# A hybrid attention and expert layer on one core: the rope tables move behind the first latents, and the first projection's weights are split ahead of tiles 2 and 3

## Chip, cores and metric

The kernel runs on one core of one Trainium2 chip. The metric is the device time of one execution in microseconds, the median of several runs.

## What is computed

One decoder layer for 512 tokens of width 1024, in fp32. This is the reference, cut to what matters here:

```python
mod = silu(c) @ w_ada + b_ada                      # 6 x 1024: shift1, scale1, gate1, shift2, scale2, gate2
h = rms_norm(x, norm1_g) * (1 + scale1) + shift1
proj = h @ w_in                                    # columns: cq 384, ckv 256, kpe 32, fq, fk, fv 512 each, fl 8
q_a = rms_norm(cq, mla_qa_g) @ w_uq                # 8 heads of 64 + 32
k_nope, v_a = rms_norm(ckv, mla_kva_g) @ w_ukv
q_a, k_a = rms_norm(q_a), rms_norm(concat(k_nope, kpe))
q_a[..., 64:], k_a[..., 64:] = rope(...)           # angles = positions * inv_freq, cos and sin
o_a = causal attention(q_a, k_a, v_a)
o_b = causal attention(fq, fk, fv) with a forget-gate bias, cumsum(log_sigmoid(fl + b_f))
x = x + gate1 * (concat(o_a, o_b) @ w_o)
h2 = rms_norm(x, norm2_g) * (1 + scale2) + shift2
x = x + gate2 * peer(h2)                           # product keys 128 x 128, 16 experts for each of 8 heads
```

## The kernel before

The 512 tokens are four tiles of 128 rows (`T[0]` to `T[3]`). The kernel is written as generators, whose order of writing is the priority of their instructions; a scheduler then gives each engine a fixed order, in which every engine works strictly. Tiles of on-chip memory come from pools with a fixed number of buffers: `k4` 28 (rows, weights), `k3` 6 (`cl`, `lT`, `macc`, `rg`, `ropework` and others), `ld` 4, `g8` 2.

Start. `setup` makes constants. `mod_cols` makes the shift `b1` and the scale `a1` of the first norm, in halves of 512 columns: eight matmuls of `w_ada` (line 303), a copy to `macc` on ScalarE (line 304), eight small matmuls that turn the row into columns (line 318), and one or two additions on VectorE (lines 319, 321). `hidden(i)` loads 128 rows of `x`, squares and sums them on ScalarE (line 345), takes the reciprocal root on GpSimd (lines 127, 128), scales on VectorE (line 347), and after a pause transposes them on the tensor engine (line 136) and applies `a1` and `b1` to each 128x128 block, even blocks on ScalarE (line 167), odd ones on VectorE (line 165). `part` then splits the result into a high part `hTh`, a cast to a reduced fp32 format on ScalarE (line 397), and a low part `hTl`, the rest (line 398: the first half on VectorE, the second on GpSimd). Before the task list starts, `hidden(0)` and `hidden(1)` and the four halves of modulation are woven by hand.

`tables` makes small constants, loads gains, and at its end calls `rope_tables`: three transfers on ScalarE's queue (`pos`, `frq`, `rg`), VectorE work on a `k3` tile `ropework` (lines 245 to 264), two sines on ScalarE (line 265), and eight products with the gains `rg` into the table `rope` (lines 274 to 277). The tables are read by GpSimd in `mla_tile` (lines 503 to 514).

Projections. `w_in(name)` loads a weight in parts of two blocks of k on SP's queue (line 371) and splits each into `whi` (ScalarE, line 373) and `wlo` (VectorE, line 374); it does so once, at its first call, and later calls find the result. `times_h` multiplies in three passes for each of 8 blocks of k: high by high, high by low, low by high (lines 385 to 387). `latent_q` uses `w_c0` (384 columns) and makes `cl`; `latent_k` uses `w_c1` (296 columns), `fox_v`, and `fox_qk` twice, use 512 columns each; `mla_tile` follows.

Order. `pipe(tasks, 3)` starts one task a step and continues each live task every third step, the newest first. The list is `hidden(2)`, `hidden(3)`, then `base`, then the heads. From step 10 on, `mods` adds the other four modulation vectors between the steps; their `w_ada` loads of 1 MB use the two `g8` buffers and are issued behind the last weight load written before them.

After the projections come attention, output projection, second norm, the product-key search, and from about 480 us on two long loops over 128 blocks of experts (`dense_u`, `v_mm`), which take most of the time.

Of the kernel before, what the change touches and what calls it, by code (L numbers as in the profile page):

```python
# [78 lines left out]
class Layer:  # L79
# [126 lines left out]
    def tables(self):  # L206
        nc, cp, I = self.nc, self.cp, self.I
        v = nc.vector
        self.io = cp.tile([P, P], F32, name="io")
        nc.gpsimd.iota(self.io, pattern=[[1, P]], base=0, channel_multiplier=0, allow_small_or_imprecise_dtypes=True)  # L210
        self.io2 = cp.tile([P, NK, 2], F16, name="io2")
        v.tensor_copy(self.io2, self.io[:, :, None].to_broadcast([P, NK, 2]))


        self.qcol_a = cp.tile([QK, 1], F32, name="qcol_a")
        self.qcol_b = cp.tile([FD + 2, 1], F32, name="qcol_b")
        g = cp.tile([ND, 4], F32, name="gcols")
        nc.scalar.dma_start(g, I["gcols"])
        v.memset(self.qcol_a, -QK ** -0.5)
        v.memset(self.qcol_b, 1.0)  # L220
        v.memset(self.qcol_b[FD:FD + 1], -1.0)
        v.scalar_tensor_tensor(out=self.qcol_a[:ND], in0=g[:, 0:1], scalar=-QK ** -0.5, in1=g[:, 1:2],
                               op0=OP.mult, op1=OP.mult)
        v.scalar_tensor_tensor(out=self.qcol_b[:FD], in0=g[:, 2:3], scalar=-FD ** -0.5, in1=g[:, 3:4],
                               op0=OP.mult, op1=OP.mult)
        self.latg = cp.tile([P, 5], F32, name="latg")
        nc.scalar.dma_start(self.latg, I["lat_g"])
        self.bf = cp.tile([P, H], F32, name="bf")
        nc.scalar.dma_start(self.bf, I["b_f"].to_broadcast([P, H]))
        self.logf = [cp.tile([P, H], F32, name=f"logf{i}") for i in range(NT)]  # L230
        self.rope_tables()

    def rope_tables(self):
        nc, cp, I = self.nc, self.cp, self.I
# [765 lines left out]
    def build(self):  # L1000
# [17 lines left out]
        def seq(*gs):  # L1018
            for g in gs:
                yield from g  # L1020
# [9 lines left out]
        def spread(g, n):  # L1030
            for _ in g:
                for _ in range(n):
                    yield
# [5 lines left out]
        def prep(f, *a):  # L1039
            f(*a)  # L1040
            yield
# [9 lines left out]
        def gates(i):  # L1051
# [1 line left out]

        every = list(range(NT))
        each = lambda f, *a: [f(i, T[i], *a) for i in every]
        base = (each(self.latent_q) + each(self.latent_k) + each(self.fox_v) + each(self.fox_qk, 0)
                + each(self.fox_qk, 1) + each(self.mla_tile))
        hs = [self.hidden(i, T[i]) for i in every]
        for x in ("a1", "b1", "a2", "b2"):
# [3 lines left out]
        h0, h1 = hs[:2]  # L1063
        for g in (m[0], h0, h1, m[1], m[0], m[2], m[1], m[3], m[2], m[3], h0, h1):
            next(g, None)
        self.tables()
        mods = spread(seq(self.mod_row(2, 0, self.g1d), self.mod_cols(3, "b2", 2), self.mod_cols(4, "a2", 3, 5),
                          self.mod_row(5, 1, self.g2d)), 2)
# [87 lines left out]
```

## Time and profile before

| | before |
|---|---|
| median of 3 runs | 1693.03 us (1692.58 to 1693.55) |
| profiled execution, its own time | 1691.5 us |
| profiled execution, its span from first to last instruction | 1689.1 us |
| mean granted tensor clock | 0.979 |
| tensor engine busy | 1586.1 us, 94% of the span |
| VectorE busy | 1263.2 us, 75% |
| ScalarE busy | 678.6 us, 40% |
| GpSimd busy | 478.6 us, 28% |

The profile shows one execution. Times in it are microseconds from the span's start. PE is the tensor engine's matmuls and PEld its weight loads, DVE is VectorE, ACT ScalarE, POOL GpSimd, SP the queue that issues most loads. A timeline row gives the start, the time it lasts, the engine and line of code, the operation, what it writes and reads, and how many instructions were merged; in brackets, how long the engine had been idle and what ended that. A granted clock of 1.00 is 2.4 GHz, 0.50 is 1.2 GHz.

### The profile page before, as it was taken

Reading aid. Unit: us, or ns where it says so; the run is one execution under the profiler, and the core shown is the slowest. Engines: PE = TensorE matmul, PEld = TensorE weight load, DVE = VectorE, ACT = ScalarE, POOL = GpSimd, SP = SyncE. Lnnn points to the kernel's source line nnn. Section 1 sums busy time; section 2 is a strip of 40 time slices with the busy share of each in tenths; the row PEclk is TensorE's granted clock in tenths of the full one; section 3 lists DMA queues with packets and bytes.
Section 4 is the critical chain, followed back from the end, with each engine's and each line's share of the span. In section 5 each row is a group of like instructions: output and inputs, shape, how many; then the busy total and the mean of one; then the engine's idle time right before and its main releaser. Section 6 shows DMA issues by size and latency. Waiting matters only on the chain.

```text
span 1689.1 us, 25030 instructions
## 1 busy us (share of the span) xinstructions
PE 1586.1 (94%) x8993; PEld 1390.9 (82%) x8993; DVE 1263.2 (75%) x2626; ACT 678.6 (40%) x1072; POOL 478.6 (28%) x514
## 2 busy tenths in 40 slices
PE   5999999998978999999999999799999999999996
PEld 2976498987977999999999999787777777877885
DVE  2624364585899679899989899488888888887863
ACT  3522364354224434334656656333333333333331
POOL 1303510001013355564213232123333333233311
PEclk8999999999989999999999999999999999999998
DMA  7354513368154688888999999999999999999852
GB/s 295 122 212 159 194 39 132 121 215 272 36 188 139 229 287 264 262 281 270 346 335 337 328 325 349 387 354 368 353 370 357 366 365 358 366 375 364 289 180 100
DMA packets 189391, 451.34 MB, mean 267 GB/s; under 512 B 16594, under 2 KB 102610, under 8 KB 185172
## 3 DMA queue, kind: packets, MB, share of 16 engines
q1 hardware_dynamic: 91732, 277.17, 46.1%
q0 software_dynamic: 38656, 139.48, 23.5%
q10 hardware_dynamic: 58880, 33.11, 6.5%
q8 instruction: 70, 1.15, 0.3%
q14 instruction: 53, 0.43, 0.1%
HBM read 393.07 MB, written 56.63 MB: 266 GB/s over the span
## 4 chain that ended last, share of the span: by engine, by line
PE 75%; DVE 11%; DMA 7%; ACT 2%; issue 2%; POOL 0%; POOLq 0%; SPq 0%; DVEq 0%; ACTq 0%
PE acc L981 27%; PE bank L937 8%; PE bank L936 8%; PE bank L935 8%; PE bank L386 4%; PE bank L173 4%; PE bank L387 4%; PE bank L385 4%; DVE ulo L872 3%; PE bank L820 3%; DMA vt<-in_peer_v 2%; PE bank L136 2%; PE bank L564 2%; PE bank L579 2%; DMA ge<-ged 1%
## 5 line engine op out<-in xcount | busy, mean ns | idle before, releaser
L981 PE MATMUL acc<-vhi,whl 128*128 128x512 f32 x1536 | 422.6, 395 | 25.7 <-ACT vhi L871 17.0
L981 PEld LDWEIGHTS acc<-vhi,whl 128*128 128x128 f32 x1536 | 289.0, 189 | 94.1 <-ACT vhi L871 21.7
L937 PE MATMUL bank<-hhi,ulo 128*128 128x384 f32 x1024 | 348.0, 340 | 17.2 <-DVE ulo L872 17.2
L935 PE MATMUL bank<-hhi,uhi 128*128 128x384 f32 x1024 | 346.3, 339 | 12.3 <-ACT uhi L871 12.2
L936 PE MATMUL bank<-hlo,uhi 128*128 128x384 f32 x1024 | 348.3, 340 | 0.0
L831 POOL DMA_INDIRECT gat<-in_peer_v,ids x128 | 158.4, 1238 | 348.2 <-DVE y L859 324.2
L871 ACT CAST uhi<-ut 128x1024 fp32r<-128x1024 f32 x128 | 134.5, 1051 | 304.5 <-PE bank L936 262.4
L981 PE MATMUL acc<-vlo,whl 128*128 128x512 f32 x768 | 241.0, 395 | 0.1
L831 POOL DMA_INDIRECT gat<-in_peer_u,ids x128 | 142.6, 1114 | 336.0 <-DVE sact L849 305.1
L872 DVE TENSOR_TENSOR ulo<-ut,uhi 128x1024 fp32r<-128x1024 f32 x128 | 178.5, 1395 | 63.6 <-ACT uhi L871 62.8
L937 PEld LDWEIGHTS bank<-hhi,ulo 128*128 128x128 f32 x1024 | 194.3, 190 | 23.0 <-DVE ulo L872 22.6
L935 PEld LDWEIGHTS bank<-hhi,uhi 128*128 128x128 f32 x1024 | 194.3, 190 | 14.2 <-ACT uhi L871 13.8
L936 PEld LDWEIGHTS bank<-hlo,uhi 128*128 128x128 f32 x1024 | 194.5, 190 | 0.5
L872 DVE TENSOR_TENSOR vlo<-vt,vhi 128x1024 fp32r<-128x1024 f32 x128 | 156.4, 1222 | 43.6 <-ACT vhi L871 42.7
L871 ACT CAST vhi<-vt 128x1024 fp32r<-128x1024 f32 x128 | 133.7, 1049 | 110.6 <-PE acc L981 85.4
L981 PEld LDWEIGHTS acc<-vlo,whl 128*128 128x128 f32 x768 | 145.1, 189 | 33.1 <-DVE vlo L872 1.2
L859 DVE SCALAR_TENSOR_TENSOR y<-gat,swgt,y 128x1024 f32<-128x1024 f32 x127 | 167.8, 1322 | 1.8 <-DMA gat<-in_peer_v,ids 1.7
L971 ACT CAST whl<-ge 128x384 fp32r<-128x384 f32 x128 | 65.4, 512 | 257.4 <-PE acc L981 240.1
L849 DVE CUSTOM_DVE_ANT_0 scr<-gat,h2r 128x1024 bf16<-128x1024 f32 x128 | 166.2, 1298 | 0.1
L972 DVE TENSOR_TENSOR whl<-ge,whl 128x384 fp32r<-128x384 f32 x128 | 70.8, 555 | 55.6 <-ACT whl L971 52.4
L822 ACT ACTIVATE gst<-bank 128x512 f32<-128x512 f32 x96 | 96.8, 1117 | 9.3 <-PE bank L820 4.7
L968 DVE TENSOR_TENSOR ge<-ge,gt 128x384 f32<-128x384 f32 x128 | 69.8, 552 | 17.7 <-DMA ge<-ged 15.6
(252 smaller groups left out, 2217.2 us busy)
## 6 DMA issues: line engine op xcount, KB each, us to landing
ut<-in_peer_uT SPq DMA_DIRECT2D x128, 512.0 KB
vt<-in_peer_v SPq DMA_DIRECT2D x128, 512.0 KB
G<-gst ACTq DMA_DIRECT2D x24, 1024.0 KB
gt<-G SPq DMA_DIRECT2D x16, 1536.0 KB
ged<-ge SPq DMA_DIRECT2D x120, 192.0 KB
ge<-ged SPq DMA_DIRECT2D x120, 192.0 KB
w<-in_w_ada SPq DMA_DIRECT2D x16, 1024.0 KB
w<-in_w_pq SPq DMA_DIRECT2D x32, 512.0 KB
```

Of the source, the lines that this page charges most:

```text
L822: nc.scalar.activation(st[:, :, q + t4:q + t4 + 4].rearrange("p i t -> p t i"), pb.rearrange("p (t i) -> p t i", t=4), AF.Copy, scale=1.0 ...
L831: self.nc.gpsimd.indirect_dma_start(out=t, out_offset=None, in_=self.I[table], in_offset=bass.IndirectOffsetOnAxis(ap=ids[:, k:k + 1], axi ...
L849: v.tensor_tensor_reduce(out=scr, in0=u, in1=self.rows, op0=OP.mult, op1=OP.add, scale=1.0, scalar=0.0, accum_out=a[:, k:k + 1])
L859: v.scalar_tensor_tensor(out=self.y, in0=t, scalar=w[:, k:k + 1], in1=self.y, op0=OP.mult, op1=OP.add)
L871: nc.scalar.copy(hi, src)
L872: self.last_split = eng.tensor_tensor(out=lo, in0=src, in1=hi, op=OP.subtract)
L935: pe.matmul(A, uh[:, k, :], hh, start=(k == 0), stop=False)
L936: pe.matmul(A, uh[:, k, :], hl, start=False, stop=False)
L937: pe.matmul(A, ul[:, k, :], hh, start=False, stop=(k == KD - 1))
L968: nc.vector.tensor_tensor(out=wg, in0=wg, in1=self.gt[:, :, b % GI, :], op=OP.mult)
L972: nc.vector.tensor_tensor(out=wl, in0=w, in1=wh, op=OP.subtract)
L981: self.nc.tensor.matmul(self.acc[t][half], w[:, ts], v[:, half * 512:(half + 1) * 512], start=(b == n == 0), stop=(b == NK - 1 and n == 2))
```

## The change

Two moves, and no instruction is added or taken away. `tables` no longer calls `rope_tables`; instead it is one more task in the list, behind the four `latent_q` and before the four `latent_k` (`prep` makes a task of one step of a plain function). And `w_in("w_c0")`, the load and split of the first projection's weight, which the first `latent_q` did at its first call, is called before `tables` and so before the tasks of `hidden(2)` and `hidden(3)`. As the list has one task more, every later task starts one step later, while `mods` still begins at step 10.

```diff
@@ tables
         self.logf = [cp.tile([P, H], F32, name=f"logf{i}") for i in range(NT)]
-        self.rope_tables()
 
@@ build
         each = lambda f, *a: [f(i, T[i], *a) for i in every]
-        base = (each(self.latent_q) + each(self.latent_k) + each(self.fox_v) + each(self.fox_qk, 0)
+        base = (each(self.latent_q) + [prep(self.rope_tables)] + each(self.latent_k) + each(self.fox_v) + each(self.fox_qk, 0)
                 + each(self.fox_qk, 1) + each(self.mla_tile))
@@ build
             next(g, None)
+        self.w_in("w_c0")
         self.tables()
```

## Rows read from the trace of the kernel before

**Rows 1.** Page, busy time: us, share of the span, instructions.
```profile
PE 1586.1 (94%) x8993; PEld 1390.9 (82%) x8993; DVE 1263.2 (75%) x2626; ACT 678.6 (40%) x1072; POOL 478.6 (28%) x514
```

**Rows 2.** Stretches from 30 to 130 us: busy per engine, clock, DMA.
```profile
30.00:32.00 2.00, 1.32 (x10) 0.97 (x8) 1.83 (x10) 0.58 (x1) 0.00 (x0) 1.00 1.03 401
32.00:42.00 10.00, 0.15 (x2) 0.10 (x1) 3.58 (x20) 5.74 (x13) 3.23 (x4) 0.54 0.32 109
42.00:46.00 4.00, 3.63 (x13) 2.80 (x14) 3.25 (x5) 1.95 (x4) 1.30 (x2) 0.50 0.03 13
46.00:63.20 17.20, 17.20 (x103) 17.17 (x102) 9.80 (x17) 8.41 (x19) 5.57 (x8) 0.99 0.41 120
63.20:72.00 8.80, 8.80 (x66) 8.80 (x66) 3.18 (x5) 2.69 (x5) 0.74 (x2) 1.00 0.93 337
72.00:130.00 58.00, 57.03 (x296) 43.43 (x298) 22.91 (x99) 19.97 (x48) 9.33 (x26) 1.00 0.42 156
```

**Rows 3.** Waits of the tensor engine, 0 to 130 us: total, times, longest.
```profile
PE bank L385 <- ACT whi L373: 10.6, 2, 9.9
```

**Rows 4.** Timeline of the tensor engine: start, duration, line, idle before.
```profile
31.00 1.05 PE L318 MATMUL bank<-o,macc 128*128 128x1 f32 x8 [0.68 <-ACT macc L304]
41.90 1.01 PE L385 MATMUL bank<-whi,hTh 128*128 128x384 f32 x2 [9.85 <-ACT whi L373]
```

**Rows 5.** Timeline of ScalarE and its queue, 30 to 76 us.
```profile
30.37 0.33 ACTq L243 DMA_DIRECT2D rg<-in_rope_g  x1
...
33.57 0.40 ACT L265 ACTIVATE ropework<-ropework 128x64 f32<-128x64 f32 x2
33.86 0.80 ACT L167 ACTIVATE x<-bank,b,a 128x128 f32<-128x128 f32 x2
37.90 1.14 ACT L397 CAST hTh<-x 128x512 fp32r<-128x512 f32 x2 [3.24 <-DVE x L165]
38.94 1.05 ACT L345 ACTIVATE xn<-x 128x1024 f32<-128x1024 f32 x1
...
41.04 0.81 ACT L373 CAST whi<-w 128x768 fp32r<-128x768 f32 x1
...
63.23 0.49 ACT L419 ACTIVATE cl<-bank 128x384 f32<-128x384 f32 x1 [3.00 <-PE bank L387]
...
74.02 1.28 ACT L450 ACT_TABLE_LOAD   x1
```

**Rows 6.** Timeline of VectorE, 30 to 68 us.
```profile
30.14 0.64 DVE L249 TENSOR_SCALAR ropework<-frq,posf 128x16 f32<-128x16 f32 x4
...
32.79 0.29 DVE L264 TENSOR_SCALAR ropework<-ropework 128x64 f32<-128x64 f32 x2
...
36.38 0.22 DVE L276 SCALAR_TENSOR_TENSOR rope<-ropework,rg 128x64 f32<-128x64 f32 x1 [2.26 <-DMA rg<-in_rope_g]
...
37.47 0.72 DVE L165 TENSOR_SCALAR x<-bank,a,b 128x128 f32<-128x128 f32 x2
42.02 0.75 DVE L347 TENSOR_SCALAR xn<-x,nrs 128x1024 f32<-128x1024 f32 x1 [3.84 <-POOL nrs L128]
...
44.17 0.95 DVE L374 TENSOR_TENSOR wlo<-w,whi 128x768 fp32r<-128x768 f32 x1
...
65.30 2.59 DVE L374 TENSOR_TENSOR wlo<-w,whi 128x592 fp32r<-128x592 f32 x3
```

**Rows 7.** Timeline of SP's queue, loads issued.
```profile
20.80 1.67 SPq L281 DMA_DIRECT2D x<-in_x  x2
...
51.49 10.76 SPq L371 DMA_DIRECT2D w<-in_w_fv  x4
62.30 32.81 SPq L291 DMA_DIRECT2D w<-in_w_ada  x4
```

**Rows 8.** Timeline of GpSimd, the low halves of `hT`.
```profile
38.59 2.49 POOL L398 TENSOR_TENSOR hTl<-x,hTh 128x512 fp32r<-128x512 f32 x2 [23.24 <-ACT hTh L397]
...
49.70 1.77 POOL L398 TENSOR_TENSOR hTl<-x,hTh 128x512 fp32r<-128x512 f32 x1 [6.24 <-ACT hTh L397]
```

## Prediction

> **What bounds the kernel now.** I began with the page's busy times: the tensor engine is busy for 94% of the span [rows 1], so time can only be won where it stands still or runs at a low clock. The stretches by window then show where that is near the change. From 30 to 32 us it is at its full clock; from 32 to 42 us it works for 0.15 us in ten, with a granted clock of 0.54; from 42 to 46 it is busy again, but at 0.50, the 1.2 GHz level; from 46 us on it is full, at 0.99 to 1.00, up to 130 us and past it [rows 2]. So there is one hole of ten microseconds ahead of the first projection, and behind it a stream that has no room. The waits of the tensor engine up to 130 us say the same: the longest ends with the first high half of `w_c0`, 9.9 us [rows 3].
>
> I then read each engine through that hole, to see which one is late. The last modulation column is made by matmuls that end at 32.05 [rows 4]. ScalarE scales its half of the first two tiles' rows at 33.86 to 34.66 and then stands idle for 3.24 us until VectorE has scaled the other half [rows 5]. VectorE is late because rope work stands in front: it waits 2.26 us for the gains `rg`, does eight table products (36.38 to 37.47) and only then scales the two rows [rows 6]. The gains were asked for at 30.37 and used 6.0 us later [rows 5, 6]. After the casts of `hTh` (37.90 to 39.04) ScalarE takes the squares of tiles 2 and 3 from 38.94, and the first high half of `w_c0` only at 41.04 [rows 5]. VectorE makes the first low half at 44.17, behind the rows of tiles 2 and 3, which begin at 42.02 [rows 6]. Rope first and later tiles second: both stand on the path that sets the hole.
>
> **The rope tables move.** Leaving the old place are fourteen VectorE instructions between 30.14 and 33.08, eight from 36.38 to 37.47, two sines in 0.40 us on ScalarE [rows 5] and three small transfers on ScalarE's queue, `pos`, `frq` and `rg`. Both engines scale blocks of the same transposed rows, so VectorE's pair could start with ScalarE's at 33.86; I allow it half a microsecond for what else stands in its order, 34.35, where the trace has 37.47 [rows 5, 6]: 3.1 us earlier (3.6 at most). The casts of `hTh` follow at 34.8 in place of 37.90.
>
> At the new place, behind the fourth `latent_q`, the same work returns: 2.9 + 1.1 = 4.0 us at most on VectorE. It is busy for 3.18 of the 8.80 us from 63.2 to 72 and 9.80 of the 17.2 before [rows 2], so the cover is 5.6 or 7.4 us. The products queue in front of whatever VectorE has next, the low halves of `w_c1` from 65.30 [rows 6], and those feed the tensor engine. In addition `rg` and `ropework` share six buffers with four `cl` tiles, so I expect them to be asked for only after the fourth `cl` is begun, at 63.23 in the old time [rows 5]; a transfer like the old one then needs 6.0 us, as its new neighbours keep the DMA engines busy at 0.93 [rows 2]. The cost is nothing if the products stand behind the low halves, and up to 6.0 us if they stand in front and the tensor engine runs dry. I take nothing for the sum, because the empty VectorE time is larger than the work, and keep 6.0 for the range.
>
> **The split of `w_c0` moves.** Four loads of 0.39 MB, four casts of 0.81 us on ScalarE and four subtractions of 0.95 us on VectorE [rows 5, 6] now stand in front of tiles 2 and 3. On SP's queue the loads pass the two rows of 0.52 MB that are issued at 20.80 [rows 7]. At 401 GB/s [rows 2] that is 2.6 us: the DMA engines fall idle at about 34.7 (109 GB/s over the ten microseconds from 32 are 2.7 us at 401), so `w_c0` is complete at about 32.1 in place of 34.7, its first two parts by 30.1, and the rows of tiles 2 and 3 come by 34.7 in place of 30.8. They are read at 38.94 [rows 5], so that is hidden; without that cover it would be 3.9 us for those two tiles alone.
>
> What is won: the two squares no longer stand before the first cast, 41.04 - 38.94 = 2.1 us. The stretch from 42 to 46 holds 13 tensor instructions; at the pace of the next stretch (103 in 17.2 us, 0.167 each) they need 2.2 us, so 1.8 of its 4 us are the low clock and the wait for the first low half. These I count as won, since ScalarE and VectorE can make both before the tensor engine comes. Third, the first four k blocks of tiles 0 and 1 are ready at 30 us, 24 matmuls of 0.167 = 4.0 us that can run while the second half is scaled. How many do depends on whether ScalarE takes the casts while it waits for the last column or behind `hTh`: between nothing and 4.0 us, and I take half, 2.0.
>
> What it costs: tile 0 and 1's last low halves, two instructions of GpSimd in 2.49 us, took 1.77 us for one when VectorE subtracted at the same time [rows 8]. With `w_c0`'s subtractions beside them I take 3.5 in place of 2.5, a loss of 1.0 us. The Trainium skill (GPSIMD Engine Reference, Specifications) says that GpSimd shares its SBUF interfaces with VectorE and contends with instructions of two SBUF inputs, which `w_c0`'s subtractions are; by that the 1.0 us is to be expected, and the 1.77 us row agrees, whereas the 2.49 us row alone would give nothing.
>
> **The queue behind.** One task more in the list puts the gate row's first two `w_ada` loads of 1 MB in front of `w_fv`'s: 5.2 us at 401 GB/s. `w_fv` is issued from 51.49 to 62.25 and `w_ada` directly behind, at 62.30 [rows 7]. The DMA engines are busy for 0.41 of the stretch from 46 to 63.2 [rows 2], so ten microseconds are free: I cost it at nothing; without that cover 5.2 us.
>
> The sum is 3.1 + 2.1 + 1.8 + 2.0 - 1.0 = 8.0 us. Everything behind hangs on the tensor engine's stream [rows 2], so it passes to the end. The profiled execution took 1691.5 us for a span of 1689.1; less 8.0 that is 1683.5. It lies 1.5 us below the median of 1693.03, so I forecast 1685.0.
>
> Bounds: the first latent matmul can't start before 32.05, against 41.90 [rows 4], 9.85 us, and with the 1.8 us that is 11.7; some room for a different order later gives 13, or 1680. The least that stands alone is the rope's 3.1 us.
>
> **The rivals.**
>
> - *Tiles 2 and 3 are late.* Their squares now follow four casts and their rows four subtractions, 3.2 and 3.8 us. If the tensor engine is through with tiles 0 and 1 before they are ready, half of the gain goes: 4 us are left, 1689. For it: VectorE waits 3.84 us for the root that GpSimd makes for tile 2, at 42.02 [rows 6], and GpSimd's last low halves of tiles 0 and 1 stand before that root. Against: all of this chain starts earlier by the rope's 3.1 us too.
> - *Rope's wait only moves.* The gains come 6.0 us after the request, VectorE holds `w_c1`'s low halves behind the products, and the tensor engine waits: 8.0 - 6.0 = 2.0 us are left, 1691, no change that can be told.
> - *The same wait drags more with it: slower.* If 6.0 us of waiting, 4.0 of work and a restart at the low clock (1.8) fall on the path in full, 11.8 us are lost against 8.0 won: 1697. It decides from 8.0 us on. It needs the low halves of `w_c1` all behind the products; against it, the row at 65.30 holds three subtractions, so at least one of the four was made before the fourth `cl` in the old order [rows 6].
> - *The sines fall behind the first exponential.* The trace has them with no table load between the last modulation columns and themselves at 33.57, and the load for the exponential at 74.02, 1.28 us [rows 5]. Behind it they would take two more loads: 2.6 us, 5.4 left, 1687.6. Their place, ten microseconds ahead of it, speaks against. The Trainium skill (ScalarE: Activation LUTs, Table sets: the hidden batching unit) asks that functions of one table set be batched, and this change moves the sines away from theirs, so by its rule the risk is real; it puts a switch at about 2.66 us, which would make 5.3 for two.
>
> **How the numbers follow.** Forecast (6 to 12 us won) 0.58; tiles 2 and 3 late 0.13; rope's wait moves 0.14; slower 0.09; sines 0.06. A measurement of this kernel tells 0.2%, 3.4 us, from no change. Faster is the first, second and last, 0.77, with 0.01 more from the rope case: 0.78; same 0.13; slower 0.09. The range runs from 1680 to 1693, which leaves out the slower case and a little below.
>
> **What would show it.** The wait before the first `w_c0` matmul falls from 9.9 us to under 3; the clock in 32 to 46 us stays near 1; VectorE's scaling stands directly behind ScalarE's; the last `latent_q` square comes at about 55 in place of 63.23; the sines show no load of their own. The prediction is wrong if VectorE waits for `rg` in front of `w_c1`, if the tensor engine has a new hole before tile 2, or if the gain at 63 us is gone at 400.

## The result, and the profile after

The median after is 1704.68 us (1703.06 to 1706.11, four runs) against 1693.29 (1692.58 to 1693.71, four runs): a ratio of 1.0068 [1.0052, 1.0084], 11.4 us slower. The forecast was 1685.0 with a range of 1680 to 1693. The profiled execution took 1705.09 us for a span of 1703.0. All times below are from its trace or from the trace of the kernel that is named; behind `tables` a line number is one lower than before.

The page's span and its busy times, which answer to [rows 1]:

```profile
span 1703.0 us, 25028 instructions
...
PE 1598.0 (94%) x8993; PEld 1398.5 (82%) x8993; DVE 1261.7 (74%) x2626; ACT 679.5 (40%) x1072; POOL 480.8 (28%) x514
```

The counts are the same, and the tensor engine is busy 11.9 us longer: 2.7 of them at the weight `w_c1`, where its clock was lower (shown below), the others spread over the span. The stretches by window, in the columns of [rows 2] (busy time of PE, PEld, DVE, ACT, POOL, then granted clock, DMA share and GB/s), show where it stands still:

```profile
20.00:32.00 12.00, 12.00 (x70) 5.75 (x71) 2.63 (x9) 3.71 (x8) 0.00 (x0) 0.73 1.03 407
32.00:42.00 10.00, 8.12 (x42) 5.88 (x39) 6.01 (x13) 6.16 (x11) 2.94 (x2) 1.00 0.39 130
42.00:52.00 10.00, 4.60 (x28) 3.89 (x26) 4.72 (x9) 5.43 (x13) 3.70 (x9) 0.91 0.35 106
52.00:62.00 10.00, 9.83 (x46) 9.73 (x47) 3.82 (x9) 4.13 (x10) 3.30 (x4) 0.74 0.58 238
62.00:72.00 10.00, 5.12 (x25) 4.78 (x24) 6.96 (x27) 3.32 (x8) 0.74 (x2) 0.77 0.34 108
72.00:82.00 10.00, 10.00 (x68) 10.00 (x67) 0.02 (x1) 0.00 (x0) 0.00 (x0) 0.89 0.00 0
```

The one hole of 32 to 42 us is closed: 8.12 us busy in ten, at 1.00, where [rows 2] has 0.15 at 0.54. In its place stand two: 4.60 busy in ten from 42 us and 5.12 from 62 us, each with a clock of 0.74 to 0.77 where work begins again. In [rows 2] the stream was full from 46 us on. The waits of the tensor engine from 30 to 130 us (total, times, longest) name the two, as [rows 3] named the one:

```profile
PE bank L384 <- ACT whi L372: 5.9, 3, 4.9
PE bank L384 <- ACT hTh L396: 3.0, 1, 3.0
PE bank L136 <- DVE xn L346: 2.5, 1, 2.5
```

The 9.9 us wait for a `whi` is gone. New are the waits for the transposes' rows `xn` (2.5 us) and for `hTh` (3.0), which are tile 2's, and a 4.9 us wait for another `whi`, that of `w_c1`. The tensor engine's timeline, as in [rows 4]:

```profile
33.52 1.05 PE L317 MATMUL bank<-o,macc 128*128 128x1 f32 x8 [0.69 <-ACT macc L303]
34.43 0.60 PE L384 MATMUL bank<-whi,hTh 128*128 128x384 f32 x2
```

The first latent matmul follows the last modulation matmuls without a wait. The modulation itself was 2.5 us later in this execution (31.00 there, 33.52 here). I put that down to the clock of the first 32 us, which differs between traces even where the work up to there is the same (last section), so I measure from the last copy of a modulation row, `macc`: 30.36 before, 32.88 after. ScalarE and its queue, as in [rows 5]:

```profile
38.37 1.14 ACT L396 CAST hTh<-x 128x512 fp32r<-128x512 f32 x2 [0.64 <-DVE x L165]
39.41 1.56 ACT L372 CAST whi<-w 128x768 fp32r<-128x768 f32 x2
44.67 0.49 ACT L418 ACTIVATE cl<-bank 128x384 f32<-128x384 f32 x1 [3.69 <-PE bank L386]
...
45.15 1.05 ACT L344 ACTIVATE xn<-x 128x1024 f32<-128x1024 f32 x1
...
46.65 1.05 ACT L344 ACTIVATE xn<-x 128x1024 f32<-128x1024 f32 x1
...
64.00 0.49 ACT L418 ACTIVATE cl<-bank 128x384 f32<-128x384 f32 x1 [3.58 <-PE bank L386]
64.01 0.33 ACTq L242 DMA_DIRECT2D rg<-in_rope_g  x1
...
67.81 0.40 ACT L264 ACTIVATE ropework<-ropework 128x64 f32<-128x64 f32 x2 [3.23 <-DVE ropework L263]
68.12 2.43 ACT L372 CAST whi<-w 128x592 fp32r<-128x592 f32 x4
...
83.04 1.28 ACT L449 ACT_TABLE_LOAD   x1
```

Read it from the top. The last casts of `w_c0` end at 40.97. Then ScalarE's order has the first latent's square, which waits 3.69 us for the tensor engine, and only behind it the squares of tiles 2 and 3: read at 45.15 and 46.65, where [rows 5] has 38.94. The engine stood idle with their rows behind it in its order. Further down, the fourth latent's square stands at 64.00, as before (63.23); behind it the sines wait 3.23 us for VectorE, and behind the sines stand all four casts of `w_c1`. VectorE, as in [rows 6]:

```profile
40.27 2.92 DVE L373 TENSOR_TENSOR wlo<-w,whi 128x768 fp32r<-128x768 f32 x2 [1.62 <-ACT whi L372]
47.23 0.75 DVE L346 TENSOR_SCALAR xn<-x,nrs 128x1024 f32<-128x1024 f32 x1 [4.04 <-POOL nrs L128]
...
61.89 0.64 DVE L248 TENSOR_SCALAR ropework<-frq,posf 128x16 f32<-128x16 f32 x4
...
65.53 0.62 DVE L420 TENSOR_SCALAR cl<-bank,rslq 128x384 f32<-128x384 f32 x1 [2.54 <-POOL rslq L128]
...
68.10 0.23 DVE L275 SCALAR_TENSOR_TENSOR rope<-ropework,rg 128x64 f32<-128x64 f32 x1 [0.22 <-ACT ropework L264]
...
69.19 2.82 DVE L373 TENSOR_TENSOR wlo<-w,whi 128x592 fp32r<-128x592 f32 x4
```

Rope begins at 61.89, but the scaling of the fourth latent is ordered into the middle of its chain and waits for GpSimd until 65.53. So the sines come at 67.81, the products at 68.10 and the low halves of `w_c1` at 69.19 (65.30 before). The gains `rg`, asked for at 64.01, are not what the products wait for: they wait 0.22 us, for ScalarE. SP's queue answers to [rows 7]:

```profile
20.06 4.22 SPq L370 DMA_DIRECT2D w<-in_w_c  x4
26.07 1.43 SPq L280 DMA_DIRECT2D x<-in_x  x2
...
49.55 0.99 SPq L290 DMA_DIRECT2D w<-in_w_ada  x2
54.92 13.19 SPq L370 DMA_DIRECT2D w<-in_w_fv  x3
86.83 0.33 SPq L280 DMA_DIRECT2D rowb<-in_rows  x1
87.25 0.38 SPq L370 DMA_DIRECT2D w<-in_w_fv  x1
```

Two `w_ada` loads have gone ahead of `w_fv`, and its last part is issued at 87.25, behind a row `rowb` at 86.83, where before all four were issued from 51.49 to 62.25. GpSimd's two last low halves of tiles 0 and 1, 2.49 us in [rows 8]:

```profile
39.06 3.31 POOL L397 TENSOR_TENSOR hTl<-x,hTh 128x512 fp32r<-128x512 f32 x2 [23.31 <-ACT hTh L396]
```

### The profile page after: what moved, and what is told of

Its sections match the earlier page's. It is cut to its first block, busy times and chain, and to the rows that moved or that the text cites. A ratio compares the mean times of both kernels' runs of the same rounds, so it can differ in the third digit from the quotient of the medians.

```text
span 1703.0 us, 25028 instructions
## 1 busy us (share of the span) xinstructions
PE 1598.0 (94%) x8993; PEld 1398.5 (82%) x8993; DVE 1261.7 (74%) x2626; ACT 679.5 (40%) x1072; POOL 480.8 (28%) x514
## 4 chain that ended last, share of the span: by engine, by line
PE 70%; DVE 16%; DMA 6%; issue 2%; ACT 2%; POOL 0%; POOLq 0%; DVEq 0%; SPq 0%; ACTq 0%
PE acc L980 26%; PE bank L936 8%; PE bank L935 8%; PE bank L934 8%; PE bank L173 4%; PE bank L385 3%; DMA vt<-in_peer_v 3%; PE bank L386 3%; PE bank L819 3%; PE bank L384 3%; DVE ulo L871 3%; PE bank L136 2%; PE bank L563 2%; PE bank L578 2%; DMA ge<-ged 2%
## 5 line engine op out<-in xcount | busy, mean ns | idle before, releaser
L936 PE MATMUL bank<-hhi,ulo 128*128 128x384 f32 x1024 | 347.9, 340 | 14.3 <-DVE ulo L871 14.1
L871 DVE TENSOR_TENSOR ulo<-ut,uhi 128x1024 fp32r<-128x1024 f32 x128 | 174.3, 1362 | 62.6 <-ACT uhi L870 61.7
```

The costliest lines, as they stand in the source:

```text
L871: self.last_split = eng.tensor_tensor(out=lo, in0=src, in1=hi, op=OP.subtract)
L936: pe.matmul(A, ul[:, k, :], hh, start=False, stop=(k == KD - 1))
```

## The experiments

Each was timed together with the kernel before on the same chip (29, 24 and 11 runs of it in the three groups; medians 1692.0, 1692.46 and 1692.39). The table cuts every span at the same events, read from the ScalarE timelines and the groups by line: the start of the last `macc` copy; from it to the fourth `latent_q` square ("start"); to the fourth `latent_k` square ("w_c1"); to the first exponential of attention ("to heads"); to the end of the span ("rest").

| kernel | last macc | start | w_c1 | to heads | rest | median us | ratio to before |
|---|---|---|---|---|---|---|---|
| before | 30.36 | 32.9 | 13.7 | 138.4 | 1473.7 | 1693.29 (beside after) | 1 |
| after | 32.88 | 31.1 | 22.6 | 141.8 | 1474.6 | 1704.68 | 1.0068 [1.0052, 1.0084] |
| wc0_only | 29.54 | 30.9 | 14.9 | 137.3 | 1476.9 | 1690.15 | 0.9982 [0.9969, 0.9995] |
| rope_only | 29.86 | 26.5 | 22.5 | 142.3 | 1469.1 | 1694.02 | 1.0016 [1.0003, 1.0029] |
| rope_own | 31.80 | 31.9 | 15.4 | 138.8 | 1474.3 | 1693.48 | 0.9999 [0.9989, 1.0008] |
| rope_later | 31.51 | 30.5 | 14.6 | 149.9 | 1474.7 | 1704.05 | 1.0068 [1.0049, 1.0087] |
| rope_old_own | 31.06 | 27.7 | 13.7 | 138.3 | 1476.1 | 1687.84 | 0.9973 [0.9963, 0.9983] |
| rope_own_same | 32.67 | 27.1 | 13.8 | 138.3 | 1472.5 | 1685.19 | 0.9958 [0.9944, 0.9973] |
| rope_same_step | 31.87 | 30.6 | 22.6 | 140.3 | 1471.4 | 1697.21 | 1.0033 [1.0020, 1.0045] |
| rows_first_own | 32.08 | 25.5 | 14.8 | 138.3 | 1473.8 | 1687.93 | 0.9976 [0.9967, 0.9986] |
| mods_11 | 30.35 | 30.5 | 22.6 | 140.2 | 1470.3 | 1698.54 | 1.0039 [1.0024, 1.0054] |
| work_own | 29.62 | 30.5 | 21.1 | 142.8 | 1471.1 | 1698.43 | 1.0040 [1.0027, 1.0053] |
| rope_own_only | 31.39 | 26.6 | 15.6 | 139.3 | 1467.5 | 1683.77 | 0.9952 [0.9939, 0.9965] |
| rows_own_same | 31.75 | 25.5 | 14.1 | 137.5 | 1472.7 | 1683.77 | 0.9945 [0.9932, 0.9958] |

The columns before "median us" are of one profiled execution each; "rest", over 1,400 us long, differs by up to 9.4 us between kernels whose code there is the same, in no order that the edits explain. What an edit does is read from the three columns ahead of it, and from the ratio.

### Each move alone

**wc0_only**: before, with only the split moved.

```diff
+        self.w_in("w_c0")
         self.tables()
```

> Only the split of w_c0 is moved; the rope tables stay in tables and the list has no task more. Theory R (the rope chain at its new place holds back the casts of w_c1, and costs some 10 us between 64 and 82 us of the trace): without that, the fourth cl comes at 63 to 65 as in the changed kernel, latent_k's first square about 9 us behind it, and the time is 1690 to 1695, near before. Theory T (the split of w_c0 ahead makes tiles 2 and 3 late, and that is the whole loss): 1700 to 1705, as with the change. Theory S (the additional list step): 1690 or less.

Measured 0.9982, 1.9 us faster. Its start is 30.9, 2.0 better than before and no worse than that of the whole change (31.1), though rope's task still stands at its old place. Its products no longer hold up the scaling there: VectorE makes them at 39.97, behind the last low halves of `w_c0`, where [rows 6] has them at 36.38 ahead of the scaling.

**rope_only**: before, with only the rope tables moved.

```diff
-        self.rope_tables()
...
-        base = (each(self.latent_q) + each(self.latent_k) + ...
+        base = (each(self.latent_q) + [prep(self.rope_tables)] + each(self.latent_k) + ...
```

> Only the rope tables are moved. Theory R: the casts of w_c1 still stand behind the sines, so the kernel is slower than before by some 5 to 8 us (10 lost, 3 won at the start): 1698 to 1701. Theory T: the rope's wait at the start is won and nothing is lost, 1688 to 1690. Theory S: as with the change, 1704.

Measured 1.0016, 2.0 us slower. Here the two sides of one move stand apart: 6.4 us won at the start (26.5), 8.8 lost at `w_c1` (22.5). The loss is there without the other move, and its size is that of the whole change (22.6). The time lies between what theory R and theory T gave: the loss is near R's 10 us, but the start wins twice the 3 us that R had. The gains don't add: 6.4 and 2.0 alone, 1.8 together.

### Which wait is lost at `w_c1`

`rg` and `ropework` are tiles of `k3`, whose six buffers the `cl` tiles use too.

**rope_own**: the change, with the two tiles in another pool that has free buffers (this edit is called "own buffers" below).

```diff
-        rg = self.k3([P, 2 * RD], "rg")
+        rg = self.k2([P, 2 * RD], "rg")
...
-        work = self.k3([P, 5, n], "ropework")
+        work = self.k2([P, 5, n], "ropework")
```

> Both moves and the same list, but rg and ropework lie in the k2 pool, which is empty at this time, so they need not wait for the fourth cl. Theory R: the tables are made early, w_c1's casts stand directly behind the third cl, and the loss between 64 and 82 us goes: 1690 to 1694. Theory T or S: 1702 to 1705, since neither depends on these buffers.

Measured 0.9999: all of the loss is gone, with both moves still in. ScalarE's timeline and queue of rope_own:

```profile
6.67 0.34 ACTq L242 DMA_DIRECT2D rg<-in_rope_g  x1
...
16.36 0.39 ACT L264 ACTIVATE ropework<-ropework 128x64 f32<-128x64 f32 x2
...
56.69 0.68 ACT L372 CAST whi<-w 128x592 fp32r<-128x592 f32 x1
...
60.00 0.68 ACT L372 CAST whi<-w 128x592 fp32r<-128x592 f32 x1
...
64.16 1.27 ACT L372 CAST whi<-w 128x592 fp32r<-128x592 f32 x2
```

The task stands at the same place in the list, but with free buffers the order of the engines brings it forward: gains at 6.67, sines at 16.36, and the casts of `w_c1` between the latents' squares. "w_c1" falls from 22.6 to 15.4. Of the 1.7 us above before that are left there, wc0_only, with rope at its old place, has 1.1 too (14.9).

**work_own**: the change, with only `ropework` in the other pool; `rg` stays in `k3`.

```diff
-        work = self.k3([P, 5, n], "ropework")
+        work = self.k2([P, 5, n], "ropework")
```

> The change as made, but only ropework lies in the k2 pool; rg stays in k3. If the sines, which stand in front of w_c1's casts on ScalarE and wait for the work in ropework, are what costs there, the sines come before 20 us, w_c1's casts come directly behind the fourth cl, at about 65, and most of the 8 us at w_c1 goes: 1694 to 1699. If the gains rg are what is waited for (my prediction's rival), it stays at 1702 to 1705.

Measured 1.0040. ScalarE of work_own, then its VectorE:

```profile
60.17 0.33 ACTq L242 DMA_DIRECT2D rg<-in_rope_g  x1
...
60.64 2.43 ACT L372 CAST whi<-w 128x592 fp32r<-128x592 f32 x4
```

```profile
63.03 0.23 DVE L273 TENSOR_TENSOR rope<-ropework,rg 128x64 f32<-128x64 f32 x1 [0.72 <-DMA rg<-in_rope_g]
...
64.12 2.83 DVE L373 TENSOR_TENSOR wlo<-w,whi 128x592 fp32r<-128x592 f32 x4
```

The sines, now at 15.62, no longer hold up the casts, which follow the fourth square at once (60.16). But `rg` is still asked for only with that square, and all four casts stand behind the request in ScalarE's order, where rope_own has two of them ahead of the square. VectorE waits 0.72 us for `rg`, and the four low halves stand behind the products. "w_c1" is 21.1, of the 7.2 us that rope_own wins there only 1.5. So both tiles have to be free; that is shown. The wait for `rg` that I had priced is small even here. What costs is the place behind the fourth square that the late request gives to casts and low halves; that last step is read from this trace and has no run of its own. The time lies in the range expected for the sines, 1694 to 1699, but not for that reason: the loss at `w_c1` stayed, and 3.5 us of the fall stand in "rest".

**rope_later**: the change, with rope behind the four `latent_k`.

```diff
-        base = (each(self.latent_q) + [prep(self.rope_tables)] + each(self.latent_k) + ...
+        base = (each(self.latent_q) + each(self.latent_k) + [prep(self.rope_tables)] + ...
```

> Both moves, but the rope task stands behind the four latent_k, so w_c1 is split first; the list is as long as with the change, and the sines now come behind the first exponential. Theory R: 1691 to 1697, the loss at w_c1 gone, 2.6 us for two more table loads. Theory T or S: 1702 to 1707.

Measured 1.0068, as slow as the change, where theory R had 1691 to 1697: it was right on "w_c1" (14.6) and missed that the way to the heads is 11.5 us longer than before. ScalarE of rope_later:

```profile
81.20 1.28 ACT L264 ACT_TABLE_LOAD   x1
82.50 0.40 ACT L264 ACTIVATE ropework<-ropework 128x64 f32<-128x64 f32 x2
```

Now the sines stand behind exponentials and take a table load of their own, and one more comes for attention's exponential at 225.28. The granted clock from 82 to 92 us is 0.50. The tables need the same buffers here, only later; how much of the 11.5 us is the buffers and how much the table loads, no run separates.

**rope_old_own**: before, with nothing moved and own buffers.

> The kernel before with one difference: rg and ropework lie in the k2 pool; no step is moved. Theory B (the whole cost of the rope tables, at either place, comes from the shared k3 buffers, which let rg be requested only after the tile ahead of it in the pool): the tables are made before 20 us, the fourth cl comes 6 to 7 us earlier than in the kernel before, as in the run with the rope moved alone (56.3 against 63.2), nothing is lost at w_c1, and the time is 1685 to 1688. Rival P (only the place in the order counts): 1692, no change.

Measured 0.9973, 4.6 us faster. `rg` is asked for at 6.4 us in place of 30.37 [rows 5], and the eight products are through at 31.5, ahead of VectorE's scaling, where [rows 6] has them from 36.38. Rope's 3.1 us at the start were thus a wait for a buffer of `k3`: with it, the request for `rg` goes out at 30.37, right behind the copy into the last `macc`, also a `k3` tile. The fourth `cl` comes 4.5 us earlier (58.76), less than the 6 to 7 expected.

### Why the start gains 1.8 and not 8

**rows_first_own**: the change with own buffers, and with the first phase of tiles 2 and 3 (load, square, root) written ahead of the split.

```diff
+        for g in hs[2:]:
+            next(g, None)
         self.w_in("w_c0")
```

> Both moves, rope in k2 buffers, and the first phase of hidden(2) and hidden(3) (rows loaded, squared and scaled) is written ahead of w_c0's split. Theory T' (w_c0's split ahead of these rows is what makes tiles 2 and 3 late, about 7 us at the fourth cl): the fourth cl comes at about 56 to 57 in place of 63.7, and the time is 1685 to 1688 in place of 1693. Rival: what holds tiles 2 and 3 is something else, and it stays at 1692 to 1694.

Measured 0.9976; against rope_own's 0.9999 it is this edit alone. The start falls from 31.9 to 25.5. The edit moves more than the first phase: a task whose first phase is done begins with its second in the list, so the transposes of tiles 2 and 3 are also written three steps earlier, ahead of the first `latent_q`. The two parts were not run apart.

**rows_own_same**: the same, and without the extra step (next part).

> All that helped, together: w_c0's split ahead but behind the rows of tiles 2 and 3, rope in k2 buffers and in the fourth latent_q's step. If the parts add, 1682 to 1685; if w_c0's split gives nothing beside the early rope tables, 1685 to 1687.

Measured 0.9945 [0.9932, 0.9958], 1683.77 us, faster than both kernels. ScalarE of rows_own_same, its tensor engine, and that engine's waits for rows between 30 and 85 us (total, times, longest):

```profile
32.23 1.06 ACT L344 ACTIVATE xn<-x 128x1024 f32<-128x1024 f32 x1
...
34.57 1.06 ACT L344 ACTIVATE xn<-x 128x1024 f32<-128x1024 f32 x1
...
37.50 0.85 ACT L372 CAST whi<-w 128x768 fp32r<-128x768 f32 x1
```

```profile
35.14 1.86 PE L136 MATMUL bank<-ident,xn 128*128 128x128 f32 x8 [1.69 <-DVE xn L346]
37.58 1.62 PE L136 MATMUL bank<-ident,xn 128*128 128x128 f32 x8 [0.58 <-DVE xn L346]
38.95 0.59 PE L384 MATMUL bank<-whi,hTh 128*128 128x384 f32 x2
```

```profile
PE bank L136 <- DVE xn L346: 2.3, 2, 1.7
```

The squares now stand at 32.23 and 34.57, ahead of the casts of `w_c0`, the transposes of tiles 2 and 3 stand ahead of the first latent, and the stream never breaks by more than 1.7 us. The first latent matmul is later than in the change (38.95 against 34.43), the fourth latent earlier: the first tile's start was not what counted.

### The extra step in the list

**rope_same_step**: the change, with rope made inside the fourth `latent_q`'s task, so that no later task moves.

```diff
+        def after_rope(g):
+            next(g, None)
+            self.rope_tables()
+            yield
+            yield from g
...
-        base = (each(self.latent_q) + [prep(self.rope_tables)] + each(self.latent_k) + ...
+        base = (each(self.latent_q)[:3] + [after_rope(self.latent_q(3, T[3]))] + each(self.latent_k) + ...
```

> The change as made, but the rope tables are made in the step of the fourth latent_q, so that the list is no longer than before. If the additional step costs something by itself (the last part of w_fv behind a load of rows on SP's queue), the time falls by 1.5 to 3.5 us to 1700.5 to 1702.5; if not, 1704.

**mods_11**: the change, with the other modulations one step later.

```diff
-            elif n >= 10:
+            elif n >= 11:
```

> The change as made, but the other modulation vectors begin at step 11 in place of 10, so that they stand against the projections as they did before. If the additional step costs because these vectors come one task too early (their loads and rows ahead of w_fv on SP's queue), the time is that of the run with the rope tables in the fourth latent_q's step, about 1697 to 1699; if the additional step costs in another way, it stays at 1703 to 1705.

Measured 1.0033 and 1.0039: they agree, and both are 5 to 6 us better than the change by the ratio; for rope_same_step that is more than the 1.5 to 3.5 us expected. In both, `w_fv` is issued whole ahead of `w_ada`, as before. "w_c1" stays at 22.6; the way to the heads is 140.3 and 140.2, against 141.8, 142.3 and 142.8 in the three kernels that have the extra step, shared buffers and rope ahead of `latent_k`. So 1.5 to 2.6 us of the difference stand there. The tensor engine's waits on the way to the heads name a cause. Every kernel in which the modulation vectors come one task early has this row (total, times, longest; here that of the change), and no other kernel has it, mods_11 included:

```profile
PE bank L317 <- ACT macc L303: 1.7, 3, 0.8
```

The matmuls of these vectors then wait for the copies that they read. For `whi` the engine waits no longer with the step than without: 1.2 us in the change, 2.4 in rope_same_step. The rest of the 5 to 6 us, some 3 to 4 us, lies in the column "rest"; since work_own, which keeps the step, has 1471.1 there too, I don't count it as the step's price.

**rope_own_same** and **rope_own_only**: before, with rope moved and own buffers, without and with the extra step.

> The rope tables are moved, with buffers of the k2 pool, into the step of the fourth latent_q, so that the list is as long as before; w_c0's split is not moved. Theory B: as with the rope tables left in place in k2 buffers, 1685 to 1688, since with early buffers the place doesn't matter. Rival P: a different time from that run by 3 us or more.

> The rope tables moved as one more task, with both buffers in the k2 pool; w_c0's split is not moved. Against the same without the additional step (1685.2): if the step costs by itself, 1688 to 1691; if it only matters together with w_c0's split, 1685 to 1686.

Measured 0.9958 and 0.9952: with free buffers and the split in its old place the ratio shows no price of the step, though `w_ada` goes ahead of `w_fv` in the second too. With free buffers and the split ahead it does: from rows_first_own to rows_own_same 0.9976 falls to 0.9945, some 5 us. The three columns don't disagree like that: the step costs 2.0 us in them from rope_same_step to the change, 1.5 from rows_own_same to rows_first_own, and 2.4 from rope_own_same to rope_own_only, whose "rest" is 5.0 us shorter. So the step costs about 2 us in all three pairs, and what differs lies in "rest", where no edit explains it. Moving rope wins little over leaving it once the buffers are free: 0.9973 in rope_old_own.

## Why the prediction was wrong

**The step that failed: rope at its new place, costed at nothing "because the empty VectorE time is larger than the work".** It measured 8.9 us. The stage between the fourth `latent_q` and the fourth `latent_k` square, before and after, in the columns of the windows:

```profile
63.23:76.97 13.74, 13.60 (x102) 13.37 (x100) 5.70 (x24) 7.27 (x22) 4.62 (x18) 1.00 0.61 222
```

```profile
64.00:86.61 22.61, 16.33 (x101) 16.02 (x101) 9.02 (x44) 7.56 (x24) 4.26 (x17) 0.85 0.15 48
```

Of 8.87 us, 6.14 are idle time of the tensor engine (22.61 - 16.33 against 13.74 - 13.60) and 2.73 nearly the same matmuls (101 against 102) at a lower clock, 0.85 against 1.00. VectorE had room for the work, 9.02 busy of 22.61, but an engine that works strictly in order doesn't use room: the chain waited for a latent in its middle, and the high halves of `w_c1` waited on another engine, ScalarE, behind the sines.

I had read that `rg` and `ropework` share buffers with `cl` and come only behind the fourth one. That was right of `rg` (64.01, with the fourth square at 64.00); the work in `ropework` begins at 61.89, behind the third latent's scaling. rope_own shows that these buffers are the cause: with others, 7.2 of the 8.9 us go. I priced the case by one wait, for `rg`, on VectorE, at 6.0 us and 0.14. In the change nothing waited for `rg`; ScalarE's order did it, sines first and the casts of `w_c1` behind them. With the sines early, the late request for `rg` keeps casts and low halves behind the fourth square (work_own), and the transfer itself takes 2.9 us there (60.17 to 63.03), not 6.0.

The case closest to the result was "the same wait drags more with it", 1697 at 0.09: 6.0 + 4.0 + 1.8 = 11.8 us against 8.9 measured at that place. It named the place and the low clock (1.8, measured 2.7), but its 6.0 us of waiting were for the wrong thing. What argued against it, a low half made ahead of the fourth `cl`, was right of the old order, where two of the four were:

```profile
58.11 1.32 DVE L374 TENSOR_TENSOR wlo<-w,whi 128x592 fp32r<-128x592 f32 x1
...
61.13 0.77 DVE L374 TENSOR_TENSOR wlo<-w,whi 128x592 fp32r<-128x592 f32 x1
```

It said nothing of the new order, which has all four at 69.19.

**The gain at the start: 8.0 forecast, 1.8 measured.** The first tiles did what was forecast and more: first latent square 24.0 us behind the last `macc` before, 11.8 after. The wait before the first `w_c0` matmul is gone and the clock from 32 to 42 us is 1.00. But the rival "tiles 2 and 3 are late" took nearly all of it, not the half that I allowed. With the split ahead the squares of tiles 2 and 3 came behind the first latent's square as well, which no row of before showed. And the terms were summed as if each held alone: wc0_only has the same 30.9 with rope in its old place, so with the split ahead rope's 3.1 us bought nothing, and rope_only won 6.4 without the split. The squares and transposes of tiles 2 and 3, moved back ahead, bring 6.4 (rope_own to rows_first_own).

**The queue behind, costed at nothing.** The DMA engines had the room, but `w_fv` lost its place to a load that waits for something else: its last part was issued at 87.25 behind `rowb`, 25 us later than before. That this delay costs is not shown: behind it the tensor engine waits no longer for a `whi` than without the step. The 1.5 to 2.6 us on the way to the heads go with the waits for `macc`, 1.7 us, which I had not looked for; my bound was 5.2. By medians the change is 5 to 6 us better without the step; where the rest of that comes from stays open.

**Right.** GpSimd's two low halves took 3.31 us (2.49 before, 3.5 forecast), and VectorE's two subtractions beside them 2.92 where one took 0.95 [rows 6]; the rule on shared SBUF interfaces in the Trainium skill (GPSIMD Engine Reference, Specifications) agrees. The rows of tiles 2 and 3 were asked for later (26.07, 20.80 before) and were hidden as transfers, for ScalarE reads them only at 45.15. The sines took no table load in the change: the only one behind them is at 83.04, as at 74.02 before. Of the signs that I had named for being wrong, the hole before tile 2 came and the wait for `rg` did not.

**The sum of the profiled execution.** Modulation later 2.5, start -1.8, `w_c1` +8.9, to the heads +3.4, rest +0.9: 13.9 us, the difference of the spans (1703.0 - 1689.1). Without the modulation's 2.5 it is 11.4. That the medians differ by 11.4 too is in part chance, for a median carries each execution's own modulation time.

## What to carry to other kernels

Before a step is moved behind others, look up which buffers its tiles come from and which tile must be done with them first: free buffers alone gave more here (0.9973) than either move, and turned the change from 1.0068 to 0.9999. When work is taken from the front of a stage, ask what the engine's fixed order puts there in its place, and follow the last tile of the stage, not the first: behind the modulation the first latent came 12 us earlier and the fourth 1.8. Idle time on an engine is cover only for work whose inputs are ready when the engine comes to it.

## What the hardware showed beside that

The granted clock from 20 to 32 us, under work that hardly differs between these kernels, was 0.90 before, 0.73 after, and 0.74 to 1.00 in the experiments; the last `macc` copy came at 29.54 to 32.88. The change and mods_11 differ only in a step that comes later, and had 0.73 and 0.89, and the last `macc` at 32.88 and 30.35. A comparison of two single traces from the span's start carries such a difference along.

A table switch on ScalarE cost the load alone in the change: the instruction ahead of it ends at 83.02, the load lasts from 83.04 to 84.32, and the exponential begins at 84.33. The Trainium skill (ScalarE: Activation LUTs, What ACT_TABLE_LOAD costs) puts a switch at about 2.66 us, load and drain; between these rows there is no room for the drain, and the measurement decides here. In rope_later the sines follow their load as closely (82.48, 82.50), but behind them ScalarE stands for 2.44 us for which the profile names nothing.
